# Three groups loaded as whole rows, and dummy matmuls ahead of the first transposes, in a row-kurtosis kernel

## The chip, the core and the metric

One core of one Trainium2 chip. The metric is the device time of one execution in microseconds (us). The profile's span, from the program's first instruction to its last, is shorter than this time: here by about 1.7 to 2.0 us. That difference is called the excess below. All times come from executions on the chip.

## The reference

```python
def reference(x: np.ndarray) -> np.ndarray:      # x: 1024 x 8192, float32
    mean = np.mean(x, axis=-1, keepdims=True)
    std = np.std(x, axis=-1, keepdims=True)
    z = (x - mean) / (std + 1e-8)
    return (np.mean(z ** 4, axis=-1) - 3).astype(np.float32)
```

The kernel reads 33.55 MB and writes 4 KB, with three passes over each element: a sum, a square about the mean, and a fourth power.

## The kernel before

It takes 16 groups of 64 rows. A group is 128 half-rows of 4096 columns, one on each partition. Five slots of 4096 columns rotate, so a group's load waits until the fourth power of the group five before it is done. Sums come from VectorE (groups 0 to 3) or from transposes on TensorE (groups 4 to 14, and most of 15). ScalarE squares about the mean; VectorE and ScalarE share the fourth power at a column that is set for each group.

```python
GROUPS = [   # halves per row, pieces of the load, columns of the fourth power on ScalarE, who sums
    (2, [4096], 1280, 'DVE'),                       # group 0
    # ... 1 to 3 alike, with 1280, 768, 1536
    (2, [2304, 1792], 640, 'PE'),                   # 4 to 7
    (2, [2304, 1792], 512, 'PE'),                   # 8 to 11
    (2, [1536, 1536, 1024], 544, 'PE'),             # 12; 13 and 14 with 640 and 384
    (2, [1536, 1280, 768, 512], 1760, 'both'),      # 15
]
BATCHES = [[0, 1, 2, 3, 4, 5, 6, 7, 8, 9, 10], [11, 12, 13, 14, 15]]

# in load(i): one DMA for each piece, all issued by SyncE
        for w in pieces:
            nc.sync.dma_start(out=xt[:, c:c + w], in_=src[:, c:c + w])
            c += w

def transposed_sums(i, w):        # 32 transposes of 128 x 128, added up in PSUM
    tps = psum.tile([P, P], f32, name="tps")
    for c in range(0, w, P):
        nc.tensor.matmul(tps, lhsT=xts[i][:, c:c + P], rhs=ident,
                         start=c == 0, stop=c == w - P, is_transpose=True)
    return tps                    # VectorE then adds pairs (red), TensorE makes the mean (mps)

def keep_busy(n):                 # dummy matmuls; before, in the tail only
    for _ in range(n):
        nc.tensor.matmul(idle, lhsT=zeros[:, :P], rhs=zeros, start=True, stop=True)

# ...
    load_next(-1)
    STEPS = [(11, 12, 13)]
    # ...
    for i in range(L):
        mean(i)
        square(i)
        if i >= 1:
            fourth_dve(i - 1, GROUPS[i - 1][2])
            load_next(i - 1)
        for f in steps.get(i, ()):
            next(f, None)         # three steps of the first batch's final sums
        fourth_act(i, 0, GROUPS[i][2])
    # ... group 15 in halves, then the last batch
```

Of the kernel before, what the change touches and what calls it, by code (L numbers as in the profile page):

```python
# [15 lines left out]
GROUPS = [  # L16
    (2, [4096], 1280, 'DVE'),
    (2, [4096], 1280, 'DVE'),
    (2, [4096], 768, 'DVE'),
    (2, [4096], 1536, 'DVE'),  # L20
    (2, [2304, 1792], 640, 'PE'),
    (2, [2304, 1792], 640, 'PE'),
    (2, [2304, 1792], 640, 'PE'),
    (2, [2304, 1792], 640, 'PE'),
    (2, [2304, 1792], 512, 'PE'),
    (2, [2304, 1792], 512, 'PE'),
    (2, [2304, 1792], 512, 'PE'),
# [13 lines left out]
def kernel(  # L41
# [93 lines left out]
    def transposed_sums(i, w):  # L135
# [4 lines that stand above are left out]
        return tps  # L140

    def pair_sums(tps):
        red = small.tile([P, P], f32, name="red")
        nc.vector.tensor_reduce(  # L144
            out=red.rearrange("p (r k) -> p r k", k=2),
            in_=tps.rearrange("p (r k) -> p r k", k=2).unsqueeze(2).to_broadcast(
                [P, P // 2, 2, 2]),
            op=AO.add, axis=AX)
        return red

    def added_halves(i, c):
        t = xts[i][:, c:]
        h = t.shape[1] // 2
        part = small.tile([P, 1], f32, name="part")
        nc.vector.tensor_tensor_reduce(  # L155
            out=junk[:, :h], in0=t[:, :h], in1=t[:, h:], scale=1.0, scalar=0.0,
            op0=AO.add, op1=AO.add, accum_out=part)
        return part


    def mean(i):
        k, pieces, _, engine = GROUPS[i]
        mps = psum.tile([P, 1], f32, name="mps")
        if engine == "DVE":
            nc.tensor.matmul(mps, lhsT=blk[k], rhs=added_halves(i, 0), start=True, stop=True)  # L165
        elif engine == "both":
            c = sum(pieces[:-1])
            tps = transposed_sums(i, c)
            part = added_halves(i, c)
            nc.tensor.matmul(mps, lhsT=blk[k], rhs=part, start=True, stop=False)  # L170
            nc.tensor.matmul(mps, lhsT=pair_sums(tps), rhs=negcol, start=False, stop=True)
        else:
            tps = transposed_sums(i, n_cols // k)
            nc.tensor.matmul(mps, lhsT=pair_sums(tps), rhs=negcol, start=True, stop=True)  # L174
        nmu = small.tile([P, 1], f32, name="nmu")
        nc.scalar.copy(nmu, mps)  # L176
        nmus[i] = nmu

    def square(i, c0=0, c1=None, second=0):
        j, s2, _ = where[i]  # L180
        t = xts[i][:, c0:c1]
        nc.scalar.activation(out=t, in_=t, func=AF.Square, bias=nmus[i],  # L182
                             accum_out=s2[:, j + second:j + second + 1])

    def fourth_act(i, c0, c1):
        j, _, quads = where[i]
        if c1 > c0:
            t = xts[i][:, c0:c1]
            nc.scalar.activation(out=t, in_=t, func=AF.Square, accum_out=quads[0][:, j:j + 1])  # L189

    def fourth_dve(i, c0, c1=None, second=0):
        j, _, quads = where[i]
        t = xts[i][:, c0:c1]
        nc.vector.tensor_tensor_reduce(  # L194
            out=t, in0=t, in1=t, scale=1.0, scalar=0.0,
            op0=AO.mult, op1=AO.add, accum_out=quads[1 + second][:, j:j + 1])
# [4 lines left out]
    def keep_busy(n):  # L201
        for _ in range(n):
            nc.tensor.matmul(idle, lhsT=zeros[:, :P], rhs=zeros, start=True, stop=True)  # L203
# [46 lines left out]
    def load_next(done):  # L250
        while to_load and held.get(SLOT_OF[to_load[0]], -1) <= done:
            i = to_load.pop(0)
            held[SLOT_OF[i]] = i
            load(i)

    load_next(-1)
    STEPS = [(11, 12, 13)]
    steps = {}
    for b, ats in zip(BATCHES[:-1], STEPS):
        f = finish(b)  # L260
        for at in ats:
            steps.setdefault(at, []).append(f)
    for i in range(L):
        mean(i)
        square(i)
        if i >= 1:
# [3 lines that stand above are left out]
            next(f, None)  # L270
        fourth_act(i, 0, GROUPS[i][2])
# [45 lines left out]
```

## Time and profile before

| | before |
|---|---|
| time, median of the first 3 runs | 97.15 us (96.98 to 97.32) |
| span of the profiled execution | 95.2 us |
| busy: ScalarE, VectorE, TensorE | 79.8, 72.7, 59.5 us |
| DMA | full from 5 us on, last landing at 84.3 us |

The prediction shows the lines of this profile and how they are read. The last landing here is that of the last load; a load has landed when all of its data have arrived. A load has landed when all 16 DMA engines have reported, and the trace holds their 16 completion signals for every load. "Typical landing" is their median below, "last landing" the latest of the 16. Only the last one releases TensorE.

### The profile page before, as it was taken

Reading aid. Unit: us, or ns where it says so; the run is one execution under the profiler, and the core shown is the slowest. Engines: PE = TensorE matmul, PEld = TensorE weight load, DVE = VectorE, ACT = ScalarE, POOL = GpSimd, SP = SyncE. Lnnn points to the kernel's source line nnn. Section 1 sums busy time; section 2 is a strip of 40 time slices with the busy share of each in tenths; the row PEclk is TensorE's granted clock in tenths of the full one; section 3 lists DMA queues with packets and bytes.
Section 4 is the critical chain, followed back from the end, with each engine's and each line's share of the span. In section 5 each row is a group of like instructions: output and inputs, shape, how many; then the busy total and the mean of one; then the engine's idle time right before and its main releaser. Section 6 shows DMA issues by size and latency. Waiting matters only on the chain.

```text
span 95.2 us, 1248 instructions
## 1 busy us (share of the span) xinstructions
PE 59.5 (62%) x450; PEld 52.5 (55%) x450; DVE 72.7 (76%) x63; ACT 79.8 (84%) x88; POOL 2.7 (3%) x12
## 2 busy tenths in 40 slices
PE   0000202001089797979796969797979797989770
PEld 0000202001089696969695959686969696874330
DVE  2003529999995294979797979897999698999970
ACT  6000099999999779999999999999999999999970
POOL 6400000000000000000000000000000000000000
PEclk9999999999999999999999999999999999999999
DMA  4799999999999999999999999999999999700000
GB/s 89 268 433 433 433 427 433 440 433 394 425 429 413 425 428 429 412 422 412 433 409 430 424 419 420 415 408 403 423 412 420 416 407 408 276 15 0 0 0 1
DMA packets 4789, 33.63 MB, mean 353 GB/s; under 512 B 560, under 2 KB 560, under 8 KB 3248
## 3 DMA queue, kind: packets, MB, share of 16 engines
q1 hardware_dynamic: 4784, 33.56, 85.6%
q8 instruction: 3, 0.05, 0.2%
q14 instruction: 2, 0.02, 0.1%
HBM read 33.55 MB, written 0.00 MB: 352 GB/s over the span
## 4 chain that ended last, share of the span: by engine, by line
PE 26%; DMA 24%; ACT 18%; DVE 18%; issue 11%; SPq 0%; DVEq 0%
DMA xt<-in_x_dram 24%; PE tps L138 21%; ACT xt L182 16%; DVE xt L194 7%; DVE junk L155 7%; DVE red L144 2%; PE mps L174 2%; ACT xt L189 1%; PE pk L240 1%; PE mps L165 1%; PE pf L232 1%; SPq L132 0%; ACT nmu L176 0%; DVE q L194 0%; PE p L222 0%
## 5 line engine op out<-in xcount | busy, mean ns | idle before, releaser
L182 ACT ACTIVATE xt<-xt,nmu 128x4096 f32<-128x4096 f32 (+1 forms) x17 | 59.8, 3516 | 0.5
L194 DVE CUSTOM_DVE_ANT_0 xt<-xt 128x3456 f32<-128x3456 f32 (+8 forms) x17 | 57.5, 3386 | 2.3 <-ACT xt L182 1.9
L138 PE MATMUL tps<-ident,xt 128*128 128x128 f32 x380 | 46.9, 282 | 0.5 <-DMA xt<-in_x_dram 0.5
L138 PEld LDWEIGHTS tps<-ident,xt 128*128 128x128 f32 x380 | 43.9, 147 | 1.8 <-DMA xt<-in_x_dram 0.9
L165 PE MATMUL mps<-part,blk 128*128 128x1 f32 x8 | 2.3, 351 | 24.8 <-DVE part L155 24.8
L155 DVE CUSTOM_DVE_ANT_0 junk<-xt 128x2048 bf16<-128x2048 f32 (+1 forms) x5 | 9.6, 1915 | 9.9 <-DMA xt<-in_x_dram 9.9
L165 PEld LDWEIGHTS mps<-part,blk 128*128 128x128 f32 x8 | 2.0, 311 | 25.0 <-issue 11.0
L189 ACT ACTIVATE xt<-xt 128x640 f32<-128x640 f32 (+7 forms) x16 | 13.9, 870 | 0.5
L176 ACT COPY nmu<-mps 128x1 f32<-128x1 f32 x16 | 2.4, 148 | 10.7 <-PE mps L165 9.4
L144 DVE TENSOR_REDUCE red<-tps 128x128 f32<-128x256 f32 x12 | 5.1, 424 | 6.7 <-PE tps L138 6.6
L174 PEld LDWEIGHTS mps<-negcol,red 128*128 128x128 f32 x22 | 3.3, 188 | 8.9 <-issue 3.3
L174 PE MATMUL mps<-negcol,red 128*128 128x1 f32 x22 | 3.9, 249 | 6.5 <-DVE red L144 5.3
L203 PE MATMUL idle<-zeros 128*128 128x512 f32 x10 | 4.8, 609 | 0.0
L182 ACT ACTIVATION_READ_ACCUMULATOR xt<-xt,nmu 128x1 f32 x17 | 3.1, 184 | 0.0
L189 ACT ACTIVATION_READ_ACCUMULATOR xt<-xt 128x1 f32 x16 | 3.0, 186 | 0.0
L203 PEld LDWEIGHTS idle<-zeros 128*128 128x128 f32 x10 | 1.7, 191 | 1.4 <-issue 1.4
L67 ACT ACT_TABLE_LOAD x1 | 1.3, 1283 | 0.8 <-PEq L301 0.8
L194 DVE DVE_READ_ACCUMULATOR2_ANT q<- 128x1 f32 x17 | 1.4, 83 | 0.0
L218 PEld LDWEIGHTS p<-s,blk 128*128 128x128 f32 x4 | 0.7, 189 | 1.2 <-ACT xt L182 0.7
L66 DVE MEMSET zeros<- 128x512 f32 x1 | 0.5, 485 | 1.0 <-PEq L301 1.0
L218 PE MATMUL p<-s,blk 128*128 128x1 f32 x4 | 0.7, 234 | 0.7 <-ACT xt L182 0.7
L240 PE MATMUL pk<-blk,q 128*5 128x64 f32 (+1 forms) x10 | 1.0, 219 | 0.0
(32 smaller groups left out, 10.5 us busy)
## 6 DMA issues: line engine op xcount, KB each, us to landing
xt<-in_x_dram SPq DMA_DIRECT2D x8, 1152.0 KB, 11.4
xt<-in_x_dram SPq DMA_DIRECT2D x4, 2048.0 KB, 14.5
xt<-in_x_dram SPq DMA_DIRECT2D x8, 896.0 KB, 13.3
xt<-in_x_dram SPq DMA_DIRECT2D x7, 768.0 KB, 11.1
xt<-in_x_dram SPq DMA_DIRECT2D x3, 512.0 KB, 12.5
xt<-in_x_dram SPq DMA_DIRECT2D x1, 640.0 KB, 12.0
xt<-in_x_dram SPq DMA_DIRECT2D x1, 384.0 KB, 12.4
xt<-in_x_dram SPq DMA_DIRECT2D x1, 256.0 KB, 11.3
```

The lines of the kernel that those rows point to most:

```text
L138: nc.tensor.matmul(tps, lhsT=xts[i][:, c:c + P], rhs=ident, start=c == 0, stop=c == w - P, is_transpose=True)
L144: nc.vector.tensor_reduce(out=red.rearrange("p (r k) -> p r k", k=2), in_=tps.rearrange("p (r k) -> p r k", k=2).unsqueeze(2).to_broadcast ...
L155: nc.vector.tensor_tensor_reduce(out=junk[:, :h], in0=t[:, :h], in1=t[:, h:], scale=1.0, scalar=0.0, op0=AO.add, op1=AO.add, accum_out=part)
L165: nc.tensor.matmul(mps, lhsT=blk[k], rhs=added_halves(i, 0), start=True, stop=True)
L174: nc.tensor.matmul(mps, lhsT=pair_sums(tps), rhs=negcol, start=True, stop=True)
L176: nc.scalar.copy(nmu, mps)
L182: nc.scalar.activation(out=t, in_=t, func=AF.Square, bias=nmus[i], accum_out=s2[:, j + second:j + second + 1])
L189: nc.scalar.activation(out=t, in_=t, func=AF.Square, accum_out=quads[0][:, j:j + 1])
L194: nc.vector.tensor_tensor_reduce(out=t, in0=t, in1=t, scale=1.0, scalar=0.0, op0=AO.mult, op1=AO.add, accum_out=quads[1 + second][:, j:j + 1])
L203: nc.tensor.matmul(idle, lhsT=zeros[:, :P], rhs=zeros, start=True, stop=True)
L218: nc.tensor.matmul(p2[:, n - 1:], lhsT=blk[k], rhs=s2[:, n - 1 + j:n + j], start=j == 0, stop=j == 1)
L240: nc.tensor.matmul(pk, lhsT=t, rhs=m, start=j == 0, stop=j == len(terms) - 1)
```

## The change

The intent: fewer, longer DMA rows for groups 4 to 6, so that loading goes faster. Their transposes can then begin only when the whole row has landed, so dummy matmuls make TensorE warm (its clock granted in full; cold is half clock) by that time. The split of the fourth power is retuned. This is the whole diff:

```diff
-    (2, [2304, 1792], 640, 'PE'),
-    (2, [2304, 1792], 640, 'PE'),
-    (2, [2304, 1792], 640, 'PE'),
-    (2, [2304, 1792], 640, 'PE'),
+    (2, [4096], 576, 'PE'),
+    (2, [4096], 576, 'PE'),
+    (2, [4096], 576, 'PE'),
+    (2, [2304, 1792], 512, 'PE'),
@@
     STEPS = [(11, 12, 13)]
+    FIRST = [g[3] for g in GROUPS].index("PE")
@@
     for i in range(L):
+        if i == FIRST - 1:
+            keep_busy(4)
         mean(i)
```

## The prediction

> **What bounds the kernel now.** I read the page first (engines, slices, queues), then the whole timeline, then fixed stretches for DMA rate and TensorE pace, then the chain and the issues.
>
> The slices of the page:
>
> ```profile
> PE   0000202001089797979796969797979797989770
> ACT  6000099999999779999999999999999999999970
> DMA  4799999999999999999999999999999999700000
> GB/s 89 268 433 433 433 427 433 440 433 394 425 429 413 425 428 429 412 422 412 433 409 430 424 419 420 415 408 403 423 412 420 416 407 408 276 15 0 0 0 1
> ```
>
> The 16 DMA engines are full from slice 2 to slice 34 (2.38 us each): the load never pauses, though each load waits for a slot. ScalarE (ACT) has one dip, slices 13 and 14. After the load come some 11 us of tail, from the last landing (issue at 73.02 plus 11.3 us to landing, so 84.3) to the end at 95.2. So three rates are nearly level: DMA, ACT and the TensorE-VectorE loop. Stretches 6 to 21 us (rows of 16 KB, one piece per group), 25 to 60 (two pieces) and 64 to 80 (mostly three):
>
> ```profile
> 6.00:21.00 15.00, 1.14 (x4) 1.00 (x4) 9.67 (x7) 9.20 (x9) 0.00 (x0) 1.00 1.01 431
> 25.00:60.00 35.00, 29.50 (x231) 27.64 (x232) 28.37 (x21) 33.47 (x36) 0.00 (x0) 1.00 1.01 422
> 64.00:80.00 16.00, 14.27 (x127) 13.21 (x126) 14.49 (x14) 15.75 (x18) 0.00 (x0) 1.00 1.02 414
> ```
>
> The last column is GB/s, beside a full DMA share each time. A group of 2.097 MB takes 2.097/0.431 = 4.87 us in one piece, 4.97 in two, 5.07 in three: 0.10 us per extra piece of 128 rows. That it is the pieces and not the busier engines I take from 21 to 26 us, where two-piece rows begin to move, TensorE is still idle and the rate is already 415.
>
> The timeline round the first transposes:
>
> ```profile
> 21.30 0.56 PE L165 MATMUL mps<-part,blk 128*128 128x1 f32 x2 [4.73 <-DVE part L155]
> 26.53 0.56 PE L165 MATMUL mps<-part,blk 128*128 128x1 f32 x2 [4.67 <-DVE part L155]
> 26.95 5.87 PE L138 MATMUL tps<-ident,xt 128*128 128x128 f32 x32
> 27.12 0.16 ACT L176 COPY nmu<-mps 128x1 f32<-128x1 f32 x1
> 32.85 0.42 DVE L144 TENSOR_REDUCE red<-tps 128x128 f32<-128x256 f32 x1 [2.92 <-PE tps L138]
> 33.64 3.69 PE L138 MATMUL tps<-ident,xt 128*128 128x128 f32 x32
> 33.81 0.16 ACT L176 COPY nmu<-mps 128x1 f32<-128x1 f32 x1 [1.09 <-PE mps L174]
> ```
>
> Group 4's 32 transposes take 5.87 us, group 5's 3.69: the first run is slow by 2.2 us. ACT, free at 32.72, waits 1.09 us for it. That is the dip, and what the dummy matmuls aim at. Later:
>
> ```profile
> 52.17 3.83 PE L138 MATMUL tps<-ident,xt 128*128 128x128 f32 x32 [0.16 <-DMA xt<-in_x_dram]
> 62.11 3.82 PE L138 MATMUL tps<-ident,xt 128*128 128x128 f32 x32 [0.17 <-DMA xt<-in_x_dram]
> ```
>
> The chain of waits carries it:
>
> ```profile
> 51.28 10.69 DMA xt<-in_x_dram
> 61.98 0.14 issue
> 62.11 3.83 PE tps L138 x32
> ```
>
> Group 11's transposes start when its first piece lands at 61.98; the same can be worked out for group 8 (issue 36.08 + 11.0 = 47.1, start 47.2) and group 9 (41.76 + 10.3 = 52.1, start 52.17). From group 11 the chain runs through transposes, sums and means to ACT's square of group 14 and the tail. ACT has slack before that: group 8's mean is ready at 52.01 and ACT copies it at 52.85 (0.84 us slack), for group 9 0.52, for group 10 0.19, for group 11 none. ACT's period of 4.64 us there beats DMA's 4.97, so ACT catches up and is then held by the data. The dip of 1.09 us is already absorbed by group 11. The end is set by when the data land.
>
> **What the Trainium skill says.** "TensorE: Matmul & The Clock Gate", Part 1 (the HAM clock gate): the array runs at 1.2 GHz until a free-running window of about 3.4 us was busy, then at 2.4, and falls back after an idle window. The trace agrees in kind: the records of transposes come about twice as slowly until 31.5 us, some 5 us after the first matmul at 26.53. The page's PEclk row does not show it (nines throughout). The same page, Part 4 (PE-mode transpose), says full rate does not engage for transposes; this trace speaks against it, as it sped up in the midst of nothing but transposes and stayed at 115 ns each (3.69/32). "DMA: Bandwidth & Descriptors", Where 436 GB/s comes from: the ceiling is 435 GB/s; the 431 of the one-piece groups stands just below it, so whole rows have nothing further to win. Same page, Why small descriptors are slow: some 3 cycles a packet, meant for small ones. Here 0.10 us per 128 packets on 16 engines is 12.5 ns for each of an engine's 8 packets, and it shows on rows of 7 to 9 KB.
>
> **The change, part by part.**
> (a) Three second pieces go: 3 x 0.10 = 0.30 us less DMA time, and two issues on SyncE for a group become one (0.4 us each, not on the path). The queue stays full: the load of group 8 is issued about 36 us, about a group before its data begin to move. So all landings from group 7 on come 0.3 us earlier. That is on the path.
> (b) Transposes of groups 4 to 6 wait for the whole row. The last pieces landed at 28.15 (group 4), 33.3 (group 5) and about 38.8 (group 6, midway between 33.3 and group 7's 44.3), from issue plus time to landing. With (a) I take 28.05, 33.1 and 38.5. Before, transposes began at 26.95, 33.64 and 38.15. Group 4 loses 1.1 us of start, group 5 nothing, group 6 0.35.
> (c) Eight dummy instructions (a 4-byte matmul shows as two) follow group 2's mean at 21.86. In the tail such dummies start 0.43 us apart (weight loads at 86.33, 86.76, 87.19), the array warm; cold I take twice, 0.86. If the array warms 3.4 to 5 us after 21.9, that is 4 to 6 cold and 4 to 2 warm: end 27.0 to 27.9, and at worst 21.9 + 8 x 0.86 = 28.8. Group 3's mean sits behind them in TensorE's order; its part is ready at 26.4. So it ends at 27.4 to 28.3 where it ended at 27.09: ACT starts square 3 by 0.3 to 1.2 us late. Before, ACT idled 1.09 us after that group, so most of this falls into the old gap.
> (d) With a warm array group 4: 28.05 + 3.7 = 31.75, sum 32.2, mean by 32.75, against 33.79 before: 1.04 us earlier. ACT is free at 33.0 to 33.9 after (c), so square 4 starts 33.2 to 34.1, against 34.00: gain 0.8 to -0.1.
> (e) Group 6: transposes 38.5 to 42.2, sum to 42.65, mean 43.15, square about 43.35 against 43.50. What is left of the gain in (d) shrinks here to 0.15 us.
> (f) The split. ACT's fourth power takes 740 ns at 640 columns and 631 at 512, so 0.05 to 0.06 us less at 576: ACT saves 3 x 0.055 + 0.11 = 0.27 us over groups 4 to 7, VectorE takes 3 x 0.065 + 0.13 = 0.33 more (3759 to 3887 ns for 128 columns). Its period, 0.46 + 3.82, stays below 4.9, so this is off the path.
> Then to the meeting point: TensorE's shortest period is 4.5 us (33.64 to 38.15). From 38.5: group 7 at 43.0, 8 at 47.55, 9 at 52.05, 10 at 56.6, where data come at 57.0 - 0.3 = 56.7. So TensorE is back on the data by group 10. ACT: square 6 43.35, 7 48.05, then 52.7, 57.3, 61.9, and 66.55 for group 11, where data allow 67.12 - 0.3 = 66.8. Both just make it.
> Sum: the end moves with the landings, -0.30 us. ACT's gains of 0.15 + 0.27 end as slack before group 11. 97.15 - 0.30 = 96.85 us.
>
> **Rivals.**
> 1. The dip is worth its size: the start-up gap of 1.09 us comes off the end, 96.1. For it: the dip is the only idle of the busiest engine. Against: the falling slack 0.84, 0.52, 0.19, 0, and a DMA share of 1.01 in the whole stretch.
> 2. The dummies run late: cold to the end at 28.8, mean 3 at 29.3 instead of 27.09, ACT 2.2 us late less the 1.09 gap, about 1.1 late at group 4; minus ACT's savings (0.27) and its slack at the meeting point, some 0.5 stays: 97.65. For it: mean 3 stands behind them in order, and the warm-up took 5 us in the trace before. The window is free-running, so executions may differ.
> 3. Waiting for whole rows cancels the DMA gain, as the three engines are level to 0.3 us: group 6 lands at 39 instead of 38.5, TensorE meets the data only after group 11, about 97.15, no change. For it: landings from group 5 to 7 were 5.5 us apart where bytes came at 4.97, so some DMA engine lags.
> 4. Larger gain: fewer pieces also lessen that lag, 0.3 more: 96.5.
>
> **Range and chances.** Rival 1 gets 4%, rival 2 12%, rival 3 25%, rival 4 14%, my sum 45%. Runs of before spread over 0.34 us. So 96.85, 8 in 10 between 96.4 and 97.4. 2% is 1.94 us: no path here reaches it. Removing the whole dip and the whole DMA gain gives 1.4, and the worst delay 1.2. Faster by over 2%: 0.02; within 2%: 0.965; slower: 0.015.
>
> **What would show it.** (a) DMA near 430 GB/s until some 36 us and the last landing at about 84.0 from 84.3. (b) Group 4's transposes starting near 28. (c) Dummies from 21.9, ending 27 to 28, mean 3 and ACT's copy late by 0.3 to 1.2 us. (d) Group 4's transposes in about 3.7 us, ACT's wait before its mean below 0.3. (e) A wait for DMA before group 6's transposes. The chain should still show a DMA landing round group 10 or 11. I am wrong if the DMA rate does not rise in groups 4 to 6, if the array is still cold at 28, or if the end moves without the last landing.

## The result, and the profile after

| | before | after |
|---|---|---|
| time, median of 6 runs | 97.06 us (96.82 to 97.32) | 96.95 us (96.88 to 97.26) |
| ratio of the fast runs | | 0.9994 (95%: 0.997 to 1.0018) |
| span of the profiled execution | 95.2 us | 95.0 us |

A ratio is the mean time of one kernel's fast runs over the mean of the other's in the same rounds, so it is not quite the ratio of the medians. Executions over 1.5% slower than the fastest of the same kernel are left out of the means. The time lies in the predicted range and 0.10 us above the point. Whether 0.30 us, 0.15 us or nothing was gained cannot be read from these six runs.

The slices of the page after, to be held against those in the prediction:

```profile
PE   0000202009969696979797969697979798989780
ACT  6000099999999999999999999999899999999980
DMA  5799999999999999999999999999999999600000
```

ScalarE's dip in slices 13 and 14 is gone. Next the stretch in which groups 4 to 6 move, the same two lines of each kernel (length, busy time of each engine, TensorE clock, DMA share, GB/s). First before, then after:

```profile
21.00:36.00 15.00, 9.42 (x60) 9.19 (x61) 12.08 (x11) 13.75 (x14) 0.00 (x0) 1.00 1.01 421
38.00:60.00 22.00, 19.24 (x163) 17.77 (x164) 19.70 (x13) 21.71 (x24) 0.00 (x0) 1.00 1.01 422
```

```profile
21.00:36.00 15.00, 12.92 (x72) 9.55 (x73) 12.09 (x11) 14.69 (x14) 0.00 (x0) 1.00 1.01 433
38.00:60.00 22.00, 19.27 (x164) 18.01 (x165) 20.05 (x14) 21.43 (x22) 0.00 (x0) 1.00 1.01 419
```

Whole rows move at 433 GB/s instead of 421, beside a busier TensorE and ScalarE. The timeline round the first transposes after:

```profile
21.72 5.46 PE L203 MATMUL idle<-zeros 128*128 128x512 f32 x8
27.01 0.28 PE L165 MATMUL mps<-part,blk 128*128 128x1 f32 x2
27.33 0.16 ACT L176 COPY nmu<-mps 128x1 f32<-128x1 f32 x1
28.23 3.71 PE L138 MATMUL tps<-ident,xt 128*128 128x128 f32 x32 [0.94 <-DMA xt<-in_x_dram]
32.95 0.16 ACT L176 COPY nmu<-mps 128x1 f32<-128x1 f32 x1
33.13 3.71 PE L138 MATMUL tps<-ident,xt 128*128 128x128 f32 x32 [0.23 <-DMA xt<-in_x_dram]
38.12 3.68 PE L138 MATMUL tps<-ident,xt 128*128 128x128 f32 x32 [0.31 <-DMA xt<-in_x_dram]
```

Group 4's transposes take 3.71 us instead of 5.87, though they start 1.28 us later. ScalarE copies the mean at 32.95 instead of 33.81, and waits no more for it. Later, group 11:

```profile
61.75 4.03 PE L138 MATMUL tps<-ident,xt 128*128 128x128 f32 x32 [0.17 <-DMA xt<-in_x_dram]
64.03 1.51 PEld L138 LDWEIGHTS tps<-ident,xt 128*128 128x128 f32 x14 [0.37 <-DMA xt<-in_x_dram]
66.39 0.35 PE L174 MATMUL mps<-negcol,red 128*128 128x1 f32 x2 [0.61 <-ACT xt L189]
```

The first piece is taken at 61.75, which is 0.36 us earlier than before (62.11). But the transposes then wait for the second piece, and the mean (66.39, before 66.54) has only 0.15 us of the 0.36. From there to VectorE's last product (92.73, before 92.90) the lead stays at 0.15 to 0.17 us. It is still 0.17 us at the last completion signal of the output's store (94.31 before, 94.14 after). Only in the closing semaphores behind that does it grow to 0.28 us (profiled spans 95.25 and 94.97): they take 0.94 us before and 0.83 after. So the profile shows a gain near the predicted one, and the time does not. Two questions follow: why is the second piece's lead so small, and where does the rest go between span and time?

### The profile page after: what moved, and what is told of

Its sections match the earlier page's. It is cut to its first block, busy times and chain, and to the rows that moved or that the text cites. A ratio compares the mean times of both kernels' runs of the same rounds, so it can differ in the third digit from the quotient of the medians.

```text
span 95.0 us, 1258 instructions
## 1 busy us (share of the span) xinstructions
PE 62.6 (66%) x458; PEld 52.4 (55%) x458; DVE 72.7 (77%) x63; ACT 79.9 (84%) x88; POOL 2.7 (3%) x12
## 4 chain that ended last, share of the span: by engine, by line
ACT 28%; DMA 27%; PE 19%; DVE 15%; issue 7%; SPq 0%; ACTq 0%; DVEq 0%
DMA xt<-in_x_dram 27%; ACT xt L182 24%; PE tps L138 15%; DVE xt L194 7%; DVE junk L155 5%; ACT xt L189 3%; PE mps L174 2%; DVE red L144 2%; PE pk L240 1%; ACT nmu L176 1%; PE pf L232 1%; SPq L132 0%; DVE q L194 0%; PE p L222 0%; DVE kr L242 0%
## 5 line engine op out<-in xcount | busy, mean ns | idle before, releaser
L194 DVE CUSTOM_DVE_ANT_0 xt<-xt 128x3584 f32<-128x3584 f32 (+9 forms) x17 | 57.8, 3404 | 0.5 <-ACT xt L182 0.2
L138 PE MATMUL tps<-ident,xt 128*128 128x128 f32 x380 | 44.7, 274 | 2.0 <-DMA xt<-in_x_dram 1.8
L138 PEld LDWEIGHTS tps<-ident,xt 128*128 128x128 f32 x380 | 41.5, 141 | 3.4 <-DMA xt<-in_x_dram 2.3
L189 ACT ACTIVATE xt<-xt 128x512 f32<-128x512 f32 (+8 forms) x16 | 13.6, 852 | 0.5
L203 PE MATMUL idle<-zeros 128*128 128x512 f32 x18 | 10.2, 713 | 0.0
L203 PEld LDWEIGHTS idle<-zeros 128*128 128x128 f32 x18 | 3.9, 232 | 4.0 <-issue 4.0
```

Of the source, the lines that this page charges most:

```text
L138: nc.tensor.matmul(tps, lhsT=xts[i][:, c:c + P], rhs=ident, start=c == 0, stop=c == w - P, is_transpose=True)
L189: nc.scalar.activation(out=t, in_=t, func=AF.Square, accum_out=quads[0][:, j:j + 1])
L194: nc.vector.tensor_tensor_reduce(out=t, in0=t, in1=t, scale=1.0, scalar=0.0, op0=AO.mult, op1=AO.add, accum_out=quads[1 + second][:, j:j + 1])
```

## The experiments

The theory at first: the landings set the end, and the slowest of 16 DMA engines sets the landings. Its rivals: the start-up gap of ScalarE is worth its size; compute that waits for whole rows gives the gain back; the DMA rate has another cause than the number of pieces. A second theory, on the excess (the difference between time and span), came after eight runs. The landings, gathered here from the completion signals of the profiled execution of each kernel, in us:

```
               group 3         group 6         group 11, 2nd   very last piece
               typical  last   typical  last   typical  last   typical  last
before          22.88   23.29   37.78   38.20   62.67   64.14   82.97   84.32
after           22.74   23.30   37.41   37.98   62.34   63.99   82.57   84.16
after_again     22.90   23.15   37.58   37.84   62.43   64.03   82.64   84.17
rows_only       22.83   23.19   37.51   37.88   62.39   63.98   82.53   84.18
dummies_only    22.84   23.31   37.74   38.23   62.61   64.22   82.83   84.40
four_pieces     22.89   23.28   38.45   38.99   63.31   64.78   83.62   85.15
fetch_early_16  22.82   23.31   37.56   39.24   62.50   64.04   82.72   84.21
quarter_sums    22.86   23.27   37.55   37.95   62.48   62.95   82.73   84.14
```

### rows_only: the change without the dummies

```diff
-        if i == FIRST - 1:
-            keep_busy(4)
```

> The changed kernel without its four early dummy matmuls; whole rows and splits stay. If the dummies matter only because group 4 now starts late: TensorE is cold at 28.2 us, the 32 transposes of group 4 take about 5.9 us instead of 3.71, ScalarE's square of group 4 starts near 35.3 instead of 33.14, and as ScalarE then needs 4.65 to 4.7 us a group while the data allow 4.97, about 0.7 us (0.5 to 1.0) of it is left at the end: 97.6 to 98.0 us. If compute has slack everywhere and only the landings count: the time of the changed kernel, 96.95.

Measured: 97.43 us median, ratio 1.0045 (1.0017 to 1.0074), mean span 95.47. Its timeline:

```profile
28.12 6.09 PE L138 MATMUL tps<-ident,xt 128*128 128x128 f32 x32 [1.13 <-DMA xt<-in_x_dram]
35.21 0.16 ACT L176 COPY nmu<-mps 128x1 f32<-128x1 f32 x1 [2.57 <-PE mps L174]
```

The transposes run cold for 6.09 us and ScalarE idles 2.57 us. Its last landings at group 11 and at the end are those of the change to 0.02 us, yet it is 0.45 us slower on average (97.46 against 97.01, the mean of 12 executions of the change). That is the expected sign and somewhat less than the expected size. Its six executions run from 97.10 to 97.97, so the loss differs from one to the next, and the profiled one (97.70) is among the worse. On average whole rows need the dummies.

### dummies_only: the dummies in the kernel before

```diff
     for i in range(L):
+        if i == 3:
+            keep_busy(4)
         mean(i)
```

> The kernel before with the four dummies ahead of group 3's mean; pieces and splits as before. Theory that the end follows the landings: ScalarE's 1.09 us gap before group 4 goes (square 4 near 33.1 instead of 34.0), no landing moves, the time stays within 0.15 us of before (97.06). Rival, that the gap is worth its size: about 0.9 us less, 96.2.

Measured: 97.13 us, ratio 1.0015 (0.9997 to 1.0034). ScalarE copies group 4's mean at 32.93 instead of 33.81, and nothing comes of it: the rival of the gap's full size is out. The two executions with a clock of 0.998 or more (97.10 and 97.34) gain nothing either, so a throttled clock has not hidden the gain. The trace has a surprise as well. Group 7, and a stretch in it (sixth column from the right on: GpSimd's busy time, its count, clock, DMA share, GB/s):

```profile
42.24 5.35 PE L138 MATMUL tps<-ident,xt 128*128 128x128 f32 x32 [0.71 <-DMA xt<-in_x_dram]
```

```profile
42.50:46.00 3.50, 3.50 (x19) 3.50 (x18) 2.94 (x2) 3.47 (x3) 0.00 (x0) 0.51 0.99 412
```

TensorE got ahead of the data, stood nearly idle from 40.0 to 42.2 us, and ran at half clock afterwards. The clock record says: granted 0.5 from 42.51 for 3.413 us. Four of its six executions show it in their mean clock (0.982), and none of the twelve of the change does (0.998 or more). So dummies without whole rows can cost TensorE its clock a few groups later, though the time shows no loss from it.

### four_pieces: the cost of a piece, multiplied

```diff
-    (2, [4096], 576, 'PE'),                        # three times
+    (2, [1024, 1024, 1024, 1024], 576, 'PE'),
```

> The changed kernel with groups 4 to 6 loaded in four pieces of 1024 columns each instead of one: nine more pieces. If a piece costs 0.09 us of every DMA engine's time, typical landings from group 7 on come 0.8 us later than in the changed kernel, the last landing too, and the end with them: about 97.7 us. If the higher rate of the whole rows had another cause (less compute beside it), landings and time stay at the changed kernel's, 96.95.

Measured: 97.53 us, ratio 1.0075 (1.0033 to 1.0116); five of its six executions were throttled (clocks 0.963 to 0.982), in the profiled one from 44.24 us on, after group 6 had landed. From group 3 to group 6 the typical landing takes 15.56 us (38.45 - 22.89), in the change 14.67, in the kernel before 14.90 (after_again and rows_only 14.68, dummies_only 14.90). That is 0.10 us for each of nine more pieces, and (14.90 - 14.67)/3 = 0.077 us for each of the three that the change took away. With the same compute beside them, more pieces load more slowly: the pieces, with their shorter rows, are the cause of the rate.

### fetch_early: a miss

```diff
+    for _ in range(32):
+        nc.tensor.matmul(idle[:, :1], lhsT=zeros[:, :P], rhs=zeros[:, :1], start=True, stop=True)
     for i in range(L):
```

> The changed kernel with 32 tiny matmuls (128 more TensorE instructions) before the first mean, where TensorE is idle. In the changed kernel one of 16 DMA engines falls 0.8 us behind the others' landings between 43 and 46.7 us and another by 1.1 us near 62 to 64, each just after a 16 KB instruction packet of 1.1 us (at 42.27 and 60.37). If these fetches cause it, they move two groups (some 9 us) earlier, to near 33 and 51, and the gap between typical and last landing opens near 34 to 36 and 52 to 55 instead. If the stragglers have another cause, the gaps stay at 43 to 46 and 62 to 64. The time should stay within 0.2 us of the changed kernel's in both.

Measured: 100.08 us, ratio 1.0315. I had taken the tiny matmuls for nearly free:

```profile
2.34 13.81 PE L265 MATMUL idle<-zeros 128*128 128x1 f32 x64 [2.34 <-ACT zeros L67]
```

64 instructions at 0.216 us each held up the first mean until 16.6 us, and ScalarE was 5 us late from the start. The packets did move (to 35.05, 54.48, 68.78 and 85.16), but here the loads waited for slots, so the landings tell nothing.

### fetch_early_16: the miss mended

The same edit with 16 instead of 32.

> The miss of fetch_early mended: 16 tiny matmuls instead of 32. There one took 0.43 us (13.8 us for 32), so 16 from 2.3 us end at 9.3, before the first mean is due at 10.9. 64 more TensorE instructions are one group's worth (4.9 us): the 16 KB instruction packets move from 42.3, 60.4 and 74.8 to about 37.4, 55.5 and 70. If these cause the stragglers, last minus typical landing rises from 0.3-0.6 to about 1 us at the landings of 39 to 42 instead of 44.9 to 46.7, and to 1.6 at those of 57 to 60 instead of 64. If not, it rises where it did. Time within 0.3 us of the changed kernel in both.

Measured: 96.94 us over four executions, of which one was slow (98.76); ratio of the fast ones 0.999 (0.9966 to 1.0013). The packets came at 37.08, 56.78 and 71.46 instead of 42.27, 60.37 and 74.84. Group 6 now lands last at 39.24, 1.25 us after its second-last engine (37.99). Such an engine, far behind the others, is called a straggler here. In the change the first such gap is at group 8's first piece (45.74, then 46.70). The second straggler shows at group 10's second piece (second-last 58.94, typical 57.43), where the change has it at group 11's (63.80, typical 62.34). Both stragglers moved with the packets.

### quarter_sums: most of TensorE's instructions taken away

```diff
+        w = 8 * P
         for c in range(0, w, P):
```

> Wrong on purpose: the transposed sums take only 8 of a group's 32 chunks, so the means of groups 4 to 15 are off and the outputs of those rows with them. It takes away 24 of 32 transposes a group, 576 of some 916 TensorE instructions, so that [...]hardly a fetch falls into the load (the first near 80 us). If fetches make the slowest DMA engine late, the last landing comes about 0.4 us after the typical one, near 83.0 us instead of 84.16. If the engines differ for another reason, it stays at 84.1 to 84.2. The time falls by about 1 us in either case (to 95.7-96.2), as ScalarE no longer waits for sums.

Measured: 98.09 us, ratio 1.0098; its means are wrong by design. The first large packet came at 69.15 instead of my 80, and up to there no engine lags: group 11's second piece lands last at 62.95, 0.47 us after the typical one, where the change has 63.99 and 1.65. After the packet one engine lags by more than 1 us again, to the very last piece (84.14). The time missed by 2 us, for this reason:

```profile
33.40:91.30 57.90, 33.72 (x131) 25.88 (x130) 50.83 (x42) 56.12 (x65) 0.00 (x0) 0.50 0.85 352
```

With so little to do TensorE ran at half clock for 58 us, and the dummies in the tail, slow now, held up the final matmuls (last statistics at 92.20 instead of 90.11).

These runs settle the stragglers. The 16 KB instruction packets, which move when TensorE gets more or fewer instructions, take about 1.1 us each, and from then on one DMA engine's part of every load comes about that much later. The last landing is then 1.3 to 1.8 us after the typical one, where it was 0.25 to 0.6 us after it before any packet. The Trainium skill, "Runtime: NRT & Kernel Launch", Instruction fetch mechanics, has blocks of 16 KiB and 256 instructions and calls the cost of crossing one "mostly hidden". The size agrees (the packets are 16,384 bytes; 64 more instructions moved them by about 5 us). Whatever it costs the fetching engine, here the loads pay for it.

### early_finish: an attempt at a better version

```diff
-BATCHES = [[0, 1, 2, 3, 4, 5, 6, 7, 8, 9, 10], [11, 12, 13, 14, 15]]
+BATCHES = [[0, 1, 2, 3, 4, 5, 6, 7, 8], [9, 10, 11, 12, 13, 14, 15]]
-    STEPS = [(11, 12, 13)]
+    STEPS = [(9, 10, 11)]
```

> The changed kernel with the first batch of final sums ending at group 8 instead of 10 and its three steps at groups 9, 10, 11 instead of 11, 12, 13. It takes 0.9 us of TensorE (0.23 + 0.21 + 0.44) and 0.37 us of ScalarE out of the stretch after group 11, where the chain runs through TensorE with a period of 4.7 us. If that stretch bounds the end, it gains until the last landing binds: 0.22 us (84.16 landed, VectorE takes it at 84.38), so about 0.2 us less than the changed kernel, 96.75. If the slowest landing of each group binds all along: no change, 96.95.

Measured: 97.04 us, ratio 1.0001 (0.9983 to 1.0018), mean span 95.05 as with the change. Freed from 0.9 us of matmuls, TensorE only waited for data again, in group 14:

```profile
78.08 2.40 PE L138 MATMUL tps<-ident,xt 128*128 128x128 f32 x20 [0.28 <-DMA xt<-in_x_dram]
```

The gain expected from the shorter chain was wrong: the landings bind. The kept traces show it more directly. In nine profiled kernels (before, after and its repeat, and all variants but those named next) the last landing comes anywhere from 84.00 to 85.15 us, and VectorE's last product starts 8.55 to 8.66 us after it in all of them. It starts later only where compute is late or was changed: rows_only 9.39, rows_4_to_8 9.28, fetch_early 9.74, fetch_early_16 8.84, quarter_sums 10.29.

### after_again: the change, in a second session

> The changed kernel as it is, for a narrower interval against before on another chip session. The prediction on record (0.30 us less) gives a ratio of 0.9969; the theory that only the slowest of the 16 DMA engines counts, whose last landing moved by 0.16 us in the two profiles (84.32 to 84.16), gives 0.9984; no effect gives 1.000.

Measured: 96.98 us, ratio 0.9998 (0.9978 to 1.0018). With the first six runs I have twelve executions of the change and, over all sessions, 34 listed ones of the kernel before, each with its span:

| mean of | executions | time | span | excess |
|---|---|---|---|---|
| before | 34 | 97.05 | 95.33 | 1.72 |
| after | 12 | 97.01 | 95.05 | 1.96 |
| dummies_only | 6 | 97.15 | 95.43 | 1.72 |
| four_pieces | 6 | 97.74 | 96.00 | 1.74 |
| rows_only | 6 | 97.46 | 95.47 | 1.99 |
| early_finish | 6 | 97.02 | 95.05 | 1.97 |
| quarter_sums | 4 | 98.08 | 96.33 | 1.75 |

The span fell by 0.28 us, near the predicted 0.30. The time fell by 0.04, because the excess grew by 0.24. It is not a matter of whole rows (quarter_sums has them) nor of the dummies (dummies_only). What sorts the kernels is the number of SyncE's instructions in the trace: 78 before, 78, 86 and 63 in the three others with a small excess, 75 in the change, rows_only and early_finish. And with 75 the trace has an 8 KB instruction packet that ends 2.2 to 2.3 us after the span, while with 78 it ends at 1.5 or 1.6, with 86 before the span's end, and with 63 none comes. (fetch_early fits with 75 instructions and 1.92 us. Two runs do not fit throughout: fetch_early_16 also has 75, but its profiled execution shows no late packet and an excess of 1.72, its two other fast ones 2.05 and 2.09; rows_4_to_8, run later, has 73, no late packet and 1.99.)

### sp_drains_4: four empty instructions on SyncE

```diff
     load_next(-1)
+    for _ in range(4):
+        nc.sync.drain()
     STEPS = [(11, 12, 13)]
```

> The changed kernel with four empty drain instructions on SyncE after the first loads, where it waits some 15 us anyway. So far: the program's span fell by 0.29 us (95.34 to 95.05, means of 12 and 12 executions), the time by 0.05, since the time exceeds the span by 1.72 us before and by 1.96 after. In traces with 1.96 an 8 KB instruction packet ends 2.2 to 2.3 us after the span's end, in those with 1.72 at 1.5 us after it or none comes. The count of SyncE's instructions sorts them (75: late; 78 and 86: early; 63: none). If that packet is SyncE's and holds up the end, 79 instructions bring it forward to about 1.4 us after the end, the excess back to 1.72 and the time to 96.75, ratio 0.997, with the span unchanged at 95.05. If the excess comes from the whole rows or the dummies themselves: it stays 1.96 and the ratio 0.9995.

Measured: 96.80 us median, ratio 0.9979 (0.996 to 0.9998). Mean time 96.78, span 95.05, excess 1.73; the packet ends 1.55 us after the span. As expected from SyncE's packet, the span did not move and the time fell by 0.23 us against the change in its own sessions, and by 0.28 against dve_memsets_4 in the same one. The packet itself, in the stretch from 95.6 to 98.0 us in slices of 0.06 us, first in the change, then with the drains:

```profile
DMA  0000000000000000000030000000000000000000
DMA  0000005000000000000000000000000000000000
```

### dve_memsets_4: the control on another engine

```diff
     load_next(-1)
+    spare = const.tile([P, 1], f32, name="spare")
+    for _ in range(4):
+        nc.vector.memset(spare, 0.0)
```

> The control to the drains: four tiny memsets on VectorE at the start (91 to 95 instructions; the kernel before has 94), SyncE untouched. If the late packet is SyncE's: the time exceeds the span by 1.96 us as in the changed kernel, and the packet ends 2.2 us after the span. If it is VectorE's: 1.72 us, and the time falls to 96.75.

Measured: 97.06 us, ratio 1.0008 (0.9987 to 1.0029), span 95.05, excess 2.01; the packet ends 2.4 us after the span. Another 8 KB packet, VectorE's by this, moved from 79.3 to 74.3 us. It is SyncE's stream that counts. The kept traces tie the time to the packet still more closely. In the six profiled executions with 75 SyncE instructions that show it, the packet ends 2.19 to 2.41 us after the span and the excess of the same execution is 1.89 to 2.11; their difference is 0.29 to 0.31 in all six (in the change 2.22 and 1.92). In the five with 78 to 86 instructions the packet ends at 1.57 or earlier and the excess stays at 1.71 to 1.74. So once the packet is late the time follows its end. Why that end lies 0.30 us beyond the excess is not shown: the trace does not say at which moment the measured time begins.

### before_drains_4: the control on the kernel before

The same four drains in the kernel before.

> The control to sp_drains_4: the same four empty drains in the kernel before (SyncE 78 to 82 instructions). There the last 8 KB packet already ends about 1.5 us after the span, inside the 1.72 us by which the time exceeds it. If the drains only move that packet, nothing changes: span 95.3, excess 1.72, time 97.05, ratio 1.000 within 0.002, and the packet ends earlier still, at about 0.8 us. If the drains help in another way (as an earlier or later issue of loads would), the time falls by 0.2 us here as well, ratio 0.998.

Measured: 97.34 us, ratio 1.0023 (1.0004 to 1.0042), excess 1.75, packet at 0.78 us after the span. The excess stayed, as expected, and the drains do not help by themselves. The mean span, though, is 95.57 instead of 95.33: a small loss that I did not expect and can explain in part only. In its profile group 4's cold transposes take 6.07 us instead of 5.87, the last landing is at 84.51 instead of 84.32, and the closing semaphores after the store take 1.06 us instead of 0.94.

### rows_4_to_8: whole rows for two more groups

```diff
-    (2, [2304, 1792], 512, 'PE'),                  # groups 7 and 8
+    (2, [4096], 512, 'PE'),
```

> The changed kernel with groups 7 and 8 as whole rows too (two more pieces gone). Typical landings from group 9 on come 2 x 0.075 = 0.15 us earlier (the piece measured 0.075 us from one to two pieces). But group 8 lands whole at about 48.8 us, its transposes run 48.9 to 52.6 instead of 47.14 to 50.83, its mean is ready near 53.8, where ScalarE copied it at 52.15: ScalarE starts group 8 about 1.6 us late and, at 4.65 us a group, is 0.5 to 0.9 us late at group 11. Span 95.5 to 95.9. If the landings alone set the end: span 94.9.

Measured: 98.53 us median of all six runs, ratio of the fast ones 1.013 (1.0076 to 1.0184). The three executions with an unthrottled clock have spans of 95.7 to 95.9, as expected. The other three ran with a mean clock of 0.98 and spans of 97.1 to 97.3 (two of them count as slow). I leave those three out of what follows. The timeline:

```profile
44.31 3.69 PE L138 MATMUL tps<-ident,xt 128*128 128x128 f32 x32 [1.40 <-DMA xt<-in_x_dram]
48.99 0.16 ACT L176 COPY nmu<-mps 128x1 f32<-128x1 f32 x1 [1.25 <-PE mps L174]
53.73 0.16 ACT L176 COPY nmu<-mps 128x1 f32<-128x1 f32 x1
```

Group 7's whole row waits for its straggler (last landing 44.17, typical 42.45), as a packet came at 42.04. ScalarE idles 1.25 us and copies group 8's mean at 53.73, 1.58 us later than in the change. The last landing is at 84.13, no earlier than with three whole rows (84.16). VectorE's last product comes 9.28 us after it instead of 8.58. Here the wait for whole rows costs more than the saved pieces give: the third rival is real, two groups further on.

The version that beats both kernels is sp_drains_4, at 96.80 us: by 0.2% against the kernel before, and against the change by comparison over sessions only.

## Why the prediction was right or wrong

**The sum nearly held in the span and failed in the time.** The step that failed is "97.15 - 0.30 = 96.85 us": it carried the gain from the profile over to the time, as if the difference between the two were fixed. The span fell by 0.28 us, the time by 0.04. The excess grew from 1.72 to 1.96 us, and four empty instructions on SyncE brought it back to 1.73. That SyncE's instruction stream moves it is shown by the drains and by the control on VectorE. That the end waits for the late packet is inferred: in six profiled executions the excess keeps a fixed distance of 0.30 us to the packet's end, but rows_4_to_8 has the large excess without such a packet in its trace. What waits lies outside the span and stays open. That the time still fell into the range is no credit to this step.

**Part (a), 0.10 us for a piece:** 0.077 in the change, 0.10 in four_pieces. So typical landings moved by 0.23 us, not 0.30. The sign in the prediction for pieces as the cause (415 GB/s from 21 to 26 us) was weak, as the DMA share there is 0.98 and one slice dips to 394; four_pieces is the test.

**"All landings from group 7 on come 0.3 us earlier":** the typical ones nearly did, but the last ones, which count, moved by about 0.15 us in the profiled pair (64.14 to 63.99, and 84.32 to 84.16). The step overlooked that a load lands with its slowest engine, 1.35 to 1.65 us behind the typical one at the end. Instruction packets cause most of this lag, as fetch_early_16 and quarter_sums show. In this pair the lag is some 0.2 us larger in the change (1.59 against 1.35 at the last piece), but 0.17 of that is there already at group 0, whose load is the same in both (0.57 against 0.40): it belongs to the execution, not to the change. Over more profiles the last landing is at 84.32, 84.40 and 84.51 with two-piece rows (before, dummies_only, before_drains_4), and at 84.00 to 84.33, mean 84.16, with three whole rows (after, after_again, rows_only, early_finish, sp_drains_4, dve_memsets_4). That is 0.25 us earlier, about as much as the typical landings moved.

**How the span fell by 0.28:** by the landings, 0.16 us in the pair and some 0.25 over more profiles, and by the closing semaphores after the store, 0.83 us in all six with three whole rows, 0.94 in before and dummies_only. I had not considered the latter, and what sets them is open. So the agreement with 0.30 is partly luck. The retuned split was never run alone; as the last product follows the last landing by 8.58 us in both kernels, no part of the gain needs it.

**Parts (b) to (d):** starts at 28.23, 33.13 and 38.12, where 28.05, 33.1 and 38.5 were written. The dummies' last instruction ended at 27.2 (27.0 to 27.9 predicted), the clock was granted in full from 25.30, and ScalarE's copy of mean 3 came 0.21 us late (0.3 to 1.2). In after_again the dummies ended at 28.0 and the copy came 0.99 us late, without harm to the span (95.0). Square 4 started at 33.14, the good end of the range.

**Part (e):** square 6 at 42.99 instead of 43.35, since group 6 had landed at 38.20 before, not at the interpolated 38.8.

**The rivals:** the first (the gap's size) is refuted by dummies_only. The second (dummies too late) cost nothing visible in the 12 executions, though they ran to 28.0 in after_again and to 28.3 in early_finish. The third (waiting for whole rows) did not spoil this change, but does so with two more groups. The fourth (0.6 us) did not occur.

**On TensorE's clock:** the prediction held that transposes bring about full rate, against the page. The trace of before confirms it (full clock granted from 31.42 us, after 4.5 us of transposes alone), and rows_only shows the cold run once more (6.09 us, then 3.69). In the change the dummies bring it about, so its 3.71 us at 28.23 shows only that transposes keep it.

**On the DMA ceiling:** the section that the prediction cites for 435 GB/s also says that the HBM side limits loads into SBUF to about 358; the 431 measured here lies well above that.

## What to carry to other kernels

A load is as late as the slowest of its DMA engines, so read the last completion signal rather than the rate. When an engine is given less to wait for, ask whether it will then stand idle long enough to lose its clock. And compare span and time over several executions before a gain of a few tenths of a microsecond is believed or given up: a handful of instructions on an engine that does nothing critical moved the time by 0.23 us here.

## What the Trainium skill lacked or had wrong

- "TensorE: Matmul & The Clock Gate", Part 4 (PE-mode transpose): it says that full rate does not engage for transposes. In the kernel before it did, in the midst of transposes alone: 32 in 5.87 us, the next 32 in 3.69, with the full clock granted from 31.42 us on.
- The same page, Part 1: it puts the fall to half clock after an idle window of about 3.4 us. Here a partly busy one was enough: in the 3.41 us before the half clock TensorE was busy for 1.54 us in dummies_only and for 1.60 in four_pieces. In quarter_sums it stayed at half clock for 58 us with eight transposes a group, busy for 33.72 of 57.90 us. How much work keeps the clock is not on the page. (The price: 3.413 us at half clock made a group's transposes 5.35 us instead of 3.69 in dummies_only.)
- "Runtime: NRT & Kernel Launch", Instruction fetch mechanics: it lacks that a block's packet takes about 1.1 us, by which one DMA engine's part of all later loads comes later (last landing 1.3 to 1.8 us after the typical one); and that four more instructions on SyncE can change the time by 0.23 us while the span stays the same.
- "DMA: Bandwidth & Descriptors", Why small descriptors are slow: it treats small rows. Here each further piece of 128 rows cost 0.077 us of loading with rows of 7 to 9 KB and 0.10 us with rows of 4 KB, beside rows of 16 KB (two pieces 421, one 433 GB/s).
